# The inverse of the DeltaNet chunk matrices: both heads of a unit in one batch per small-tile step

## The chip, the cores and the metric

The kernel runs on one core of a Trainium2 chip. The core has a matrix engine (TensorE, in profiles PE, with its weight loads as PEld), a vector engine (VectorE, DVE), an activation engine (ScalarE, ACT), a general engine (GpSimd, POOL) and DMA queues, here nearly all issued by SyncE (SP). The engines run their own instruction streams, each in order, and wait for each other through semaphores. Matrix products read SBUF and write PSUM; DVE and ACT bring results from PSUM back to SBUF, which is called an eviction here. The metric is the device time of one execution in microseconds (us).

## What is computed

One decoder layer on 512 tokens of width 2048, in float32. An input projection of the normalised tokens (2048 by 20528) feeds two token mixers, an mLSTM of 8 heads and a gated DeltaNet of 16 heads; an output projection, two sigmoid merge gates, the residual and a final normalisation follow. This is the part of the reference that the change lies in:

```python
    decay_mat = jnp.where(incl, jnp.exp(jnp.where(incl, rel, 0.0)), 0.0)
    kk = jnp.einsum('cbhtd,cbhsd->cbhts', kc, kc)
    a_mat = jnp.where(strict, bc[..., :, None] * kk * decay_mat, 0.0)
    lhs = a_mat + jnp.eye(CHUNK, dtype=a_mat.dtype)
    ...
    sol = lax.linalg.triangular_solve(lhs, rhs, left_side=True, lower=True, unit_diagonal=True)
    w_val, w_k = sol[..., :dv], sol[..., dv:]
    ...
    def step(S, inp):
        wv, wk, qk_c, qd, ke, ge = inp
        u = wv - jnp.einsum('bhtd,bhde->bhte', wk, S)
        o = jnp.einsum('bhtd,bhde->bhte', qd, S) + jnp.einsum('bhts,bhse->bhte', qk_c, u)
        S_new = ge[..., None, None] * S + jnp.einsum('bhsd,bhse->bhde', ke, u)
        return S_new, o
```

For each head and chunk a unit lower triangular matrix has to be inverted (or solved against). The kernel does this with chunks of 128 tokens, so each head has four matrices of 128 by 128.

## The kernel before

**The stream of projections.** The kernel keeps the whole normalised input in SBUF, split in a high and a low part (uh, ul), and streams the weights through in 256 KB pieces. ACT makes the high part of a piece (`wh`, L112), DVE the low part (`wl`, L115), three pieces ahead of use. Each projection product is three TensorE products of 128x512 (L211, L212, L213: high by high, high by low, low by high). TensorE's order is written out by hand: the program issues instructions to it in program order. The other engines are ordered by a scheduler with priorities.

**Ticks.** After each six 128x512 products (or their equal) the projection loop calls `tick()`. All other TensorE work is written as Python generators that are resumed by ticks: a generator does one step's products, requests the evictions and yields the number of ticks after which it wants to go on. So a step's products stand between two projection products, and its eviction has that many ticks before the next step reads it. Every eviction that a later step needs is issued with raised priority (`urgent`).

**Units.** Twelve units follow each other: four mLSTM units ("m") and eight DeltaNet units ("d"), each of two heads, in the order m d d m d d m d d m d d; then come the merge gates and the output projection. A DeltaNet unit projects k, q, v and z for its two heads (64 ticks). `dn_front_k` and `dn_front_q` run beside its own projections: the norms (transposes pkt and pqt), the products k by k and k by q (pk, pqk), and the inverses of the 32x32 diagonal blocks of both heads' eight matrices, solved together on DVE (L530, L532) and brought through DRAM into `tn` (the inverses) and `tt` (their transposes). When the unit's projections are over, `dn_back` starts, beside the projections of the next unit.

**`dn_back` in the kernel before** runs once per head; the second head's generator starts one tick after the first's. It first transposes v (pvt, eviction into `vn`). Then it puts the block inverse together, from 32x32 blocks to 64x64 and then 128x128, in four steps, which use 32x32 and 64x64 tiles of the array:
- p1 (L597): two products a chunk, on two different 32x32 tiles; ACT evicts the negated result into `s1` (L602, one instruction for each of the two partition ranges).
- p2 (L608, L609): three products a chunk, on three different 32x32 tiles; ACT copies two results into `tb` (L613), DVE the third into `ta` (L615).
- p3 (L619): one product a chunk, all on the same 64x64 tile; ACT evicts it into `s3` (L622).
- p4 (L626): one product a chunk, all on the same 64x64 tile; DVE evicts it into `tb` (L628).

Two ticks lie between steps. `tb` then holds the transposed inverse for all four chunks. A float32 product appears as two records in the profile, a transpose as one. There are two sets of `tb` and `ta`, one for each head; POOL puts the diagonal blocks in (L589, L592).

The second half of `dn_back` is the recurrence over the four chunks: pr and the first half of po (state by k and q), the eviction `r` (DVE, L644), pw (L649, reads `tb`), its eviction `w` (ACT, L652), pst and po, the new state (DVE, L660 or L662), two ticks apart each. At the end the result is normalised (squares on ACT, POOL's power `rsd` L676, DVE's multiply `os` L679), transposed seven ticks later (pot, L683) and multiplied by the gate on DVE (`gz`, L686).

PSUM is shared by pools: `psj` (3 tiles) for projections, `psw` (3 tiles, tag "wk") for all the small results, handed out in turn, and `pso` (2 tiles) for po. A small step that gets a "wk" tile waits until the work three tiles back has been evicted.

Of the kernel before, what the change touches and what calls it, by code (L numbers as in the profile page):

```python
# [47 lines left out]
def hybrid_block(  # L48
# [119 lines left out]
    def urgent(level=1):  # L168
        return tc.high_priority(offset=level * PRIO)
# [242 lines left out]
        V.tensor_copy(acol, pc[:, :, 0:8])  # L412
        V.tensor_copy(emcol, pc[:, :, 8:16])

    NYP, NTB = 3, 2
    yps, tbs, tas = [], [], []
    for i in range(NYP):
        t = wk.tile([P, S + 3], F32, tag=f"yp{i}", name=f"yp{i}", bufs=1)
        G.memset(t[:, 0:3], 0.0)
        yps.append(t)  # L420
    for i in range(NTB):
        t = wk.tile([P, NC, P], F32, tag=f"tb{i}", name=f"tb{i}", bufs=1)
        G.memset(t, 0.0)
        tbs.append(t)
        t = wk.tile([64, NC, 64], F32, tag=f"ta{i}", name=f"ta{i}", bufs=1)
        G.memset(t, 0.0)
        tas.append(t)
    cnt = {"yp": 0, "tb": 0}

    def row_bcast(r, name):  # L430
        t = wk.tile([P, NC, P], F32, tag="rb", name=name, bufs=3)
# [134 lines left out]
            u["qt"].append(qt)  # L566
            yield 1

    def dn_back(j, hs, kq, u):
        h = hs[j]  # L570
        aq, qt, ke, ge = u["aq"][j], u["qt"][j], u["ke"][j], u["dm"][j][2]
        nk, qe = u["nk"], u["qe"]

        pv = psw.tile([P, NC, P], F32, tag="wk", name="pvt")
        for c in range(NC):
            T.transpose(pv[:, c, :], u["vt"][j][:, c * P:(c + 1) * P], ident)
        vn = wk.tile([P, NC, P], F32, tag="vn", name="vn", bufs=4)
        with urgent():
            V.tensor_tensor(out=vn, in0=pv, in1=bc(nk[:, j, :], P), op=ALU.mult)
        yield 1  # L580


        tnj, ttj = u["tn"][:, j * NC:(j + 1) * NC, :], u["tt"][:, j * NC:(j + 1) * NC, :]
        tb = tbs[cnt["tb"] % NTB]
        ta = tas[cnt["tb"] % NTB]
        cnt["tb"] += 1
        for b in range(4):
            bs = slice(b * BS, (b + 1) * BS)
            G.tensor_copy(tb[bs, :, bs], ttj[bs])  # L589
        for b in range(2):  # L590
            bs = slice(b * BS, (b + 1) * BS)
            G.tensor_copy(ta[bs, :, bs], tnj[bs])  # L592
        p1 = psw.tile([P, NC, BS], F32, tag="wk", name="p1")
        for q in range(2):
            a0, a1 = slice(64 * q, 64 * q + 32), slice(64 * q + 32, 64 * q + 64)
            for c in range(NC):
                T.matmul(p1[a1, c, :], aq[a0, c, 0, a1], tnj[a0, c, :], start=True, stop=True)  # L597
        s1 = wk.tile([P, NC, BS], F32, tag="s3", name="s1")
        for q in range(2):
            a1 = slice(64 * q + 32, 64 * q + 64)  # L600
            with urgent():
                A.mul(s1[a1], p1[a1], -1.0)  # L602
        yield 2
        p2 = psw.tile([P, 2, NC, BS], F32, tag="wk", name="p2")
        for c in range(NC):
            for q in range(2):
                a0, a1 = slice(64 * q, 64 * q + 32), slice(64 * q + 32, 64 * q + 64)
                T.matmul(p2[a0, 0, c, :], s1[a1, c, :], ttj[a1, c, :], start=True, stop=True)  # L608
            T.matmul(p2[32:64, 1, c, :], ttj[32:64, c, :], s1[32:64, c, :], start=True, stop=True)  # L609
        for q in range(2):  # L610
            a0, a1 = slice(64 * q, 64 * q + 32), slice(64 * q + 32, 64 * q + 64)
            with urgent():
                A.copy(tb[a0, :, a1], p2[a0, 0])  # L613
        with urgent():
            V.tensor_copy(ta[32:64, :, 0:32], p2[32:64, 1])  # L615
        yield 2
        p3 = psw.tile([P, NC, 64], F32, tag="wk", name="p3")
        for c in range(NC):
            T.matmul(p3[64:128, c, :], aq[0:64, c, 0, 64:128], ta[:, c, :], start=True, stop=True)  # L619
        s3 = wk.tile([P, NC, 64], F32, tag="s3", name="s3")  # L620
        with urgent():
            A.mul(s3[64:128], p3[64:128], -1.0)  # L622
        yield 2
        p4 = psw.tile([P, NC, 64], F32, tag="wk", name="p4")
        for c in range(NC):
            T.matmul(p4[0:64, c, :], s3[64:128, c, :], tb[64:128, c, 64:128], start=True, stop=True)  # L626
        with urgent():
            V.tensor_copy(tb[0:64, :, 64:128], p4[0:64])  # L628
        yield 2


        po = pso.tile([P, NC, P], F32, tag="o", name="po")
        ssq = wk.tile([P, NC], F32, tag="ssq", name="ssq")
        st = None
        for c in range(NC):
            tsl = slice(c * P, (c + 1) * P)
            if st is None:
                r = vn[:, c, :]
            else:
                pr = psw.tile([P, P], F32, tag="wk", name="pr")  # L640
                T.matmul(pr, kq[j][:, 0, tsl], st, start=True, stop=True)
                r = wk.tile([P, P], F32, tag="r", name="r")
                with urgent():
                    V.scalar_tensor_tensor(out=r, in0=pr, scalar=negeg[:, c, h:h + 1], in1=vn[:, c, :],  # L644
                                           op0=ALU.mult, op1=ALU.add)
                T.matmul(po[:, c, :], qt[:, c, :], st, start=True, stop=False)
                yield 2
            pw = psw.tile([P, P], F32, tag="wk", name="pw")
            T.matmul(pw, tb[:, c, :], r, start=True, stop=True)  # L649
            w = wk.tile([P, P], F32, tag="w", name="w")  # L650
            with urgent():
                A.copy(w, pw)  # L652
            yield 2
            if c < NC - 1:
                pst = psw.tile([P, P], F32, tag="wk", name="pst")
                T.matmul(pst, ke[:, c, :], w, start=True, stop=True)
                sn = wk.tile([P, P], F32, tag="st", name="st", bufs=4)
                with urgent():
                    if st is None:
                        V.tensor_copy(sn, pst)  # L660
                    else:
                        V.scalar_tensor_tensor(out=sn, in0=st, scalar=ge[:, c:c + 1], in1=pst,  # L662
                                               op0=ALU.mult, op1=ALU.add)
            T.matmul(po[:, c, :], aq[:, c, 1, :], w, start=(st is None), stop=True)
            if c < NC - 1:
                st = sn
                yield 2

        jk = wk.tile([P, P], F32, tag="jk", name="jk", bufs=1)
        for c in range(NC):  # L670
            with urgent():
                A.activation(jk, po[:, c, :], AF.Square, accum_out=ssq[:, c:c + 1])
        with urgent():
            V.scalar_tensor_tensor(out=ssq, in0=ssq, scalar=1.0 / P, in1=qe[:, j, :], op0=ALU.mult, op1=ALU.add)
        rsd = wk.tile([P, NC], F32, tag="rsd", name="rsd")
        G.tensor_tensor(out=rsd, in0=ssq, in1=mhalf, op=ALU.pow)  # L676
        os_ = wk.tile([P, NC, P], F32, tag="os", name="os")
        with urgent():
            V.tensor_tensor(out=os_, in0=po, in1=bc(rsd, P), op=ALU.mult)  # L679
        yield 7  # L680
        pt = psw.tile([P, S], F32, tag="wk", name="pot")
        for c in range(NC):
            T.transpose(pt[:, c * P:(c + 1) * P], os_[:, c, :], ident)  # L683
        ht = u["g"][j]
        with urgent():
            V.scalar_tensor_tensor(out=ht, in0=pt, scalar=normc[:, 32:33], in1=ht, op0=ALU.mult, op1=ALU.mult)  # L686
        nc.sync.dma_start(h_d[KT + h], ht)

    def dn_unit(p):
        hs = (2 * p, 2 * p + 1)  # L690
        dcol = p * NB
        u = {"aq": [], "qt": [], "ke": [], "vt": [], "g": [], "dm": []}
        kq = [wk.tile([P, 2, S], F32, tag="kq", name=f"kq{h}", bufs=4) for h in hs]
        ps = proj_cm(DN_K + dcol)
        for j in range(2):
            conv_silu(ps[j], 16 + hs[j], kq[j][:, 0, :])
        start(dn_front_k(hs, kq, u), KWAIT)
        ps = proj_cm(DN_Q + dcol)
        for j in range(2):
            conv_silu(ps[j], hs[j], kq[j][:, 1, :])  # L700
        start(dn_front_q(hs, kq, u), QWAIT)
        ps = proj_cm(DN_V + dcol)
        for j in range(2):
            vt = wk.tile([P, S], F32, tag="vn", name="vt", bufs=4)
            conv_silu(ps[j], 32 + hs[j], vt)
            u["vt"].append(vt)
        ps = proj_cm(DN_Z + dcol)
        for j in range(2):
            g = wk.tile([P, S], F32, tag="g", name="gz", bufs=4)
            silu2(ps[j], g)  # L710
            u["g"].append(g)
        start(dn_back(0, hs, kq, u), 4)
        start(dn_back(1, hs, kq, u), 5)

    def ml_prep(j, hs, kq, u):
        h = hs[j]
# [280 lines left out]
```

## Time and profile before

| what | value |
|---|---|
| median of 3 runs | 2379.36 us (2378.52 to 2379.41) |
| the profiled execution | 2379.44 us, span 2377.7 us |
| mean granted TensorE clock | 0.998 |
| TensorE (PE) busy | 2344.2 us, 99% of the span |
| DVE, ACT, POOL busy | 1145.5, 826.5, 237.0 us |
| DMA | 265.94 MB, mean 112 GB/s |

The profile is of one execution. The span is from its first to its last instruction; the time of the execution is 1.7 us longer. A group line gives busy time and the mean duration of one instruction; a wait line gives the total, the count and the longest; a timeline line gives the start, the duration, the engine, the line of the kernel, and the idle time before it with what ended it. Products overlap each other, so the pitch of a stream is read from starts, not from durations.

### The profile page before, as it was taken

Reading aid. Unit: us, or ns where it says so; the run is one execution under the profiler, and the core shown is the slowest. Engines: PE = TensorE matmul, PEld = TensorE weight load, DVE = VectorE, ACT = ScalarE, POOL = GpSimd, SP = SyncE. Lnnn points to the kernel's source line nnn. Section 1 sums busy time; section 2 is a strip of 40 time slices with the busy share of each in tenths; the row PEclk is TensorE's granted clock in tenths of the full one; section 3 lists DMA queues with packets and bytes.
Section 4 is the critical chain, followed back from the end, with each engine's and each line's share of the span. In section 5 each row is a group of like instructions: output and inputs, shape, how many; then the busy total and the mean of one; then the engine's idle time right before and its main releaser. Section 6 shows DMA issues by size and latency. Waiting matters only on the chain. (4 is left out here: it accounts for less than half of the span.)

```text
span 2377.7 us, 32465 instructions
## 1 busy us (share of the span) xinstructions
PE 2344.2 (99%) x11999; PEld 1953.4 (82%) x11999; DVE 1145.5 (48%) x2307; ACT 826.5 (35%) x1854; POOL 237.0 (10%) x319
## 2 busy tenths in 40 slices
PE   6999999999999999999999999999999999999998
PEld 5888888888888888888888888888998888888886
DVE  5433767433485833348583324958333222434334
ACT  5323434332343423243343224433333323322222
POOL 0000212100021210011220002112000000010010
PEclk9999999999999999999999999999999999999999
DMA  5433334333333333333342333333375544634333
GB/s 147 114 96 102 94 100 100 94 98 98 98 94 98 107 89 98 97 94 98 96 120 74 107 97 92 96 93 103 91 233 147 159 115 122 207 114 128 121 115 129
DMA packets 232354, 265.94 MB, mean 112 GB/s; under 512 B 46337, under 2 KB 171490, under 8 KB 232194
## 3 DMA queue, kind: packets, MB, share of 16 engines
q1 hardware_dynamic: 232130, 263.79, 39.1%
q8 instruction: 94, 1.54, 0.3%
q14 instruction: 66, 0.54, 0.1%
q10 hardware_dynamic: 64, 0.07, 0.0%
HBM read 239.61 MB, written 24.18 MB: 111 GB/s over the span
## 5 line engine op out<-in xcount | busy, mean ns | idle before, releaser
L115 DVE TENSOR_TENSOR wl<-wr,wh 128x512 fp32r<-128x512 f32 x768 | 550.1, 718 | 875.3 <-ACT wh L112 850.3
L112 ACT CAST wh<-wr 128x512 fp32r<-128x512 f32 x768 | 475.7, 621 | 1148.5 <-PE pj L212 565.4
L211 PE MATMUL pj<-uh,wh 128*128 128x512 f32 x1792 | 736.4, 411 | 2.1 <-ACT yp L442 1.6
L213 PE MATMUL pj<-uh,wl 128*128 128x512 f32 x1792 | 701.4, 391 | 0.0
L212 PE MATMUL pj<-ul,wh 128*128 128x512 f32 x1792 | 699.9, 391 | 0.0
L213 PEld LDWEIGHTS pj<-uh,wl 128*128 128x128 f32 x1792 | 336.5, 188 | 74.5 <-DVE wl L115 0.4
L211 PEld LDWEIGHTS pj<-uh,wh 128*128 128x128 f32 x1792 | 337.4, 188 | 67.1 <-ACT yp L442 2.9
L212 PEld LDWEIGHTS pj<-ul,wh 128*128 128x128 f32 x1792 | 337.9, 189 | 60.5
L935 PE MATMUL py<-wh,hh 128*128 128x512 f32 x512 | 199.2, 389 | 0.0
L936 PE MATMUL py<-wl,hh 128*128 128x512 f32 x512 | 199.2, 389 | 0.0
L937 PE MATMUL py<-wh,hl 128*128 128x512 f32 x512 | 199.2, 389 | 0.0
L241 PE MATMUL pg<-wh,uh 128*128 128x512 f32 x384 | 149.4, 389 | 0.0
L242 PE MATMUL pg<-wl,uh 128*128 128x512 f32 x384 | 149.4, 389 | 0.0
L243 PE MATMUL pg<-wh,ul 128*128 128x512 f32 x384 | 149.4, 389 | 0.0
L936 PEld LDWEIGHTS py<-wl,hh 128*128 128x128 f32 x512 | 96.1, 188 | 20.1
L935 PEld LDWEIGHTS py<-wh,hh 128*128 128x128 f32 x512 | 96.1, 188 | 20.0
L937 PEld LDWEIGHTS py<-wh,hl 128*128 128x128 f32 x512 | 96.1, 188 | 19.8
L241 PE MATMUL pv<-wh,uh 128*128 128x512 f32 x256 | 99.6, 389 | 0.0
L242 PE MATMUL pv<-wl,uh 128*128 128x512 f32 x256 | 99.6, 389 | 0.0
L243 PE MATMUL pv<-wh,ul 128*128 128x512 f32 x256 | 99.6, 389 | 0.0
L530 DVE TENSOR_TENSOR tmp<-ls,xi 32x31 f32<-32x31 f32 (+15 forms) x248 | 91.1, 367 | 5.2 <-DMA ls<-ld 1.7
L532 DVE TENSOR_TENSOR xi<-xi,tmp 32x31 f32<-32x31 f32 (+15 forms) x248 | 87.0, 351 | 4.0
(249 smaller groups left out, 2457.8 us busy)
## 6 DMA issues: line engine op xcount, KB each, us to landing
wr<-in_w_in_dram SPq DMA_DIRECT2D x640, 256.0 KB, 2.8
wr<-in_w_out_dram SPq DMA_DIRECT2D x128, 256.0 KB, 3.1
hr<-h_d SPq DMA_DIRECT2D x32, 256.0 KB, 3.5
tgl<-tg_d SPq DMA_DIRECT2D x32, 256.0 KB, 3.3
tg_d<-tgw SPq DMA_DIRECT2D x24, 256.0 KB, 3.8
xt<-in_x_dram SPq DMA_DIRECT2D x8, 512.0 KB, 9.0
gb<-rows_d SPq DMA_DIRECT2D x16, 256.0 KB, 3.4
h_d<-mg SPq DMA_DIRECT2D x16, 256.0 KB, 3.1
```

The lines of the kernel that those rows point to most:

```text
L112: A.copy(hi, src)
L115: V.tensor_tensor(out=lo, in0=src, in1=hi.bitcast(F32), op=ALU.subtract)
L211: T.matmul(ps[j], hi[:, k, wsl], uh[:, kt, :], start=(kt == 0), stop=False)
L212: T.matmul(ps[j], hi[:, k, wsl], ul[:, kt, :], start=False, stop=False)
L213: T.matmul(ps[j], lo[:, k, wsl], uh[:, kt, :], start=False, stop=(kt == KT - 1))
L241: T.matmul(ps[c], uh[:, kt, tsl], hi[:, 0, :], start=(kt == 0), stop=False)
L242: T.matmul(ps[c], uh[:, kt, tsl], lo[:, 0, :], start=False, stop=False)
L243: T.matmul(ps[c], ul[:, kt, tsl], hi[:, 0, :], start=False, stop=(kt == KT - 1))
L530: V.tensor_tensor(out=tv, in0=ls[:, i, i + 1:BS].unsqueeze(2).to_broadcast([NSYS, n, m]), in1=xi[:, i, 0:m].unsqueeze(1).to_broadcast([NSY ...
L935: T.matmul(ps[c], hh[base][:, kt, tsl], hi[:, 0, :], start=(kt == 0), stop=False)
L936: T.matmul(ps[c], hh[base][:, kt, tsl], lo[:, 0, :], start=False, stop=False)
L937: T.matmul(ps[c], hl[base][:, kt, tsl], hi[:, 0, :], start=False, stop=(kt == KT - 1))
```

## The change

The four steps p1 to p4 are done for both heads of a unit at once. `dn_back` becomes one generator for the unit. It transposes v of head 0 and, a tick later, of head 1; then each of the four steps issues the products of both heads' eight matrices (index `g`) into one PSUM tile and evicts them with the same number of instructions as one head had before, each twice as wide. In p1 the products go to the two array tiles in turn for each matrix, where before all of one tile came first. `tb` and `ta` are single tiles of twice the size, `s1` and `s3` share one buffer. After p4 two generators `dn_chain` are started, one for each head, 2 and 3 ticks later; they hold the recurrence and the rest of the old `dn_back`, unchanged except for the index into `tb`.

```diff
-    NYP, NTB = 3, 2
...
-    for i in range(NTB):
-        t = wk.tile([P, NC, P], F32, tag=f"tb{i}", name=f"tb{i}", bufs=1)
...
+    tb = wk.tile([P, 2 * NC, P], F32, tag="tb", name="tb", bufs=1)
+    G.memset(tb, 0.0)
+    ta = wk.tile([64, 2 * NC, 64], F32, tag="ta", name="ta", bufs=1)
+    G.memset(ta, 0.0)
...
-    def dn_back(j, hs, kq, u):
+    def dn_back(hs, kq, u):
+        u["vs"] = []
+        for j in range(2):
+            pv = psw.tile([P, NC, P], F32, tag="wk", name="pvt")
...
+            u["vs"].append(vn)
+            yield 1
+        tn, tt = u["tn"], u["tt"]
+        G2 = [(j * NC + c, u["aq"][j][:, c, 0, :]) for j in range(2) for c in range(NC)]
...
-        p1 = psw.tile([P, NC, BS], F32, tag="wk", name="p1")
-        for q in range(2):
-            a0, a1 = slice(64 * q, 64 * q + 32), slice(64 * q + 32, 64 * q + 64)
-            for c in range(NC):
-                T.matmul(p1[a1, c, :], aq[a0, c, 0, a1], tnj[a0, c, :], start=True, stop=True)
-        s1 = wk.tile([P, NC, BS], F32, tag="s3", name="s1")
+        p1 = psw.tile([P, 2 * NC, BS], F32, tag="wk", name="p1")
+        for g, a in G2:
+            for q in range(2):
+                a0, a1 = slice(64 * q, 64 * q + 32), slice(64 * q + 32, 64 * q + 64)
+                T.matmul(p1[a1, g, :], a[a0, a1], tn[a0, g, :], start=True, stop=True)
+        s1 = wk.tile([P, 2 * NC, BS], F32, tag="s3", name="s1", bufs=1)
...
+        p2 = psw.tile([P, 2, 2 * NC, BS], F32, tag="wk", name="p2")
+        for g, a in G2:
+            for q in range(2):
+                a0, a1 = slice(64 * q, 64 * q + 32), slice(64 * q + 32, 64 * q + 64)
+                T.matmul(p2[a0, 0, g, :], s1[a1, g, :], tt[a1, g, :], start=True, stop=True)
+            T.matmul(p2[32:64, 1, g, :], tt[32:64, g, :], s1[32:64, g, :], start=True, stop=True)
...
+        p3 = psw.tile([P, 2 * NC, 64], F32, tag="wk", name="p3")
+        for g, a in G2:
+            T.matmul(p3[64:128, g, :], a[0:64, 64:128], ta[:, g, :], start=True, stop=True)
...
+        p4 = psw.tile([P, 2 * NC, 64], F32, tag="wk", name="p4")
+        for g, a in G2:
+            T.matmul(p4[0:64, g, :], s3[64:128, g, :], tb[64:128, g, 64:128], start=True, stop=True)
+        with urgent():
+            V.tensor_copy(tb[0:64, :, 64:128], p4[0:64])
+        start(dn_chain(0, hs, kq, u), 2)
+        start(dn_chain(1, hs, kq, u), 3)
+
+    def dn_chain(j, hs, kq, u):
...
-            T.matmul(pw, tb[:, c, :], r, start=True, stop=True)
+            T.matmul(pw, tb[:, j * NC + c, :], r, start=True, stop=True)
...
-        start(dn_back(0, hs, kq, u), 4)
-        start(dn_back(1, hs, kq, u), 5)
+        start(dn_back(hs, kq, u), 4)
```

More of the change, by code (lines that the diff above doesn't have):

```diff
@@ L413, in gates @@
         V.tensor_copy(emcol, pc[:, :, 8:16])
-    NYP, NTB = 3, 2
-    yps, tbs, tas = [], [], []
+    NYP = 3
+    yps = []
     for i in range(NYP):
@@ L420, in hybrid_block @@
         yps.append(t)
-    for i in range(NTB):
-        t = wk.tile([P, NC, P], F32, tag=f"tb{i}", name=f"tb{i}", bufs=1)
[L423 to L428, printed above, removed]
+    tb = wk.tile([P, 2 * NC, P], F32, tag="tb", name="tb", bufs=1)
+    G.memset(tb, 0.0)
+    ta = wk.tile([64, 2 * NC, 64], F32, tag="ta", name="ta", bufs=1)
+    G.memset(ta, 0.0)
+    cnt = {"yp": 0}
     def row_bcast(r, name):
@@ L567, in dn_front_q @@
             yield 1
-    def dn_back(j, hs, kq, u):
[L570 to L574, printed above, removed]
-        for c in range(NC):
[L576 to L586, printed above, removed]
+    def dn_back(hs, kq, u):
+        u["vs"] = []
+        for j in range(2):
+            pv = psw.tile([P, NC, P], F32, tag="wk", name="pvt")
+            for c in range(NC):
+                T.transpose(pv[:, c, :], u["vt"][j][:, c * P:(c + 1) * P], ident)
+            vn = wk.tile([P, NC, P], F32, tag="vn", name="vn", bufs=4)
+            with urgent():
+                V.tensor_tensor(out=vn, in0=pv, in1=bc(u["nk"][:, j, :], P), op=ALU.mult)
+            u["vs"].append(vn)
+            yield 1
+        tn, tt = u["tn"], u["tt"]
+        G2 = [(j * NC + c, u["aq"][j][:, c, 0, :]) for j in range(2) for c in range(NC)]
@@ L587, in dn_back @@
         for b in range(4):
             bs = slice(b * BS, (b + 1) * BS)
-            G.tensor_copy(tb[bs, :, bs], ttj[bs])
+            G.tensor_copy(tb[bs, :, bs], tt[bs])
         for b in range(2):
             bs = slice(b * BS, (b + 1) * BS)
-            G.tensor_copy(ta[bs, :, bs], tnj[bs])
-        p1 = psw.tile([P, NC, BS], F32, tag="wk", name="p1")
-        for q in range(2):
-            a0, a1 = slice(64 * q, 64 * q + 32), slice(64 * q + 32, 64 * q + 64)
-            for c in range(NC):
-                T.matmul(p1[a1, c, :], aq[a0, c, 0, a1], tnj[a0, c, :], start=True, stop=True)
@@ L598, in dn_back @@
-        s1 = wk.tile([P, NC, BS], F32, tag="s3", name="s1")
+            G.tensor_copy(ta[bs, :, bs], tn[bs])
+        p1 = psw.tile([P, 2 * NC, BS], F32, tag="wk", name="p1")
[4 more added lines that the diff above has]
+        s1 = wk.tile([P, 2 * NC, BS], F32, tag="s3", name="s1", bufs=1)
         for q in range(2):
@@ L603, in dn_back @@
         yield 2
-        p2 = psw.tile([P, 2, NC, BS], F32, tag="wk", name="p2")
-        for c in range(NC):
+        p2 = psw.tile([P, 2, 2 * NC, BS], F32, tag="wk", name="p2")
+        for g, a in G2:
             for q in range(2):
                 a0, a1 = slice(64 * q, 64 * q + 32), slice(64 * q + 32, 64 * q + 64)
-                T.matmul(p2[a0, 0, c, :], s1[a1, c, :], ttj[a1, c, :], start=True, stop=True)
-            T.matmul(p2[32:64, 1, c, :], ttj[32:64, c, :], s1[32:64, c, :], start=True, stop=True)
+                T.matmul(p2[a0, 0, g, :], s1[a1, g, :], tt[a1, g, :], start=True, stop=True)
+            T.matmul(p2[32:64, 1, g, :], tt[32:64, g, :], s1[32:64, g, :], start=True, stop=True)
         for q in range(2):
@@ L616, in dn_back @@
         yield 2
[L617 to L620, printed above, removed]
+        p3 = psw.tile([P, 2 * NC, 64], F32, tag="wk", name="p3")
+        for g, a in G2:
+            T.matmul(p3[64:128, g, :], a[0:64, 64:128], ta[:, g, :], start=True, stop=True)
+        s3 = wk.tile([P, 2 * NC, 64], F32, tag="s3", name="s3", bufs=1)
         with urgent():
@@ L623, in dn_back @@
         yield 2
-        p4 = psw.tile([P, NC, 64], F32, tag="wk", name="p4")
-        for c in range(NC):
-            T.matmul(p4[0:64, c, :], s3[64:128, c, :], tb[64:128, c, 64:128], start=True, stop=True)
+        p4 = psw.tile([P, 2 * NC, 64], F32, tag="wk", name="p4")
+        for g, a in G2:
+            T.matmul(p4[0:64, g, :], s3[64:128, g, :], tb[64:128, g, 64:128], start=True, stop=True)
         with urgent():
             V.tensor_copy(tb[0:64, :, 64:128], p4[0:64])
-        yield 2
+        start(dn_chain(0, hs, kq, u), 2)
+        start(dn_chain(1, hs, kq, u), 3)
+    def dn_chain(j, hs, kq, u):
+        h = hs[j]
+        aq, qt, ke, ge = u["aq"][j], u["qt"][j], u["ke"][j], u["dm"][j][2]
+        qe, vn = u["qe"], u["vs"][j]
         po = pso.tile([P, NC, P], F32, tag="o", name="po")
```

## The prediction

> **What bounds the kernel now.** I read the page first: busy time per engine, and the forty slices.
>
> ```profile
> PE 2344.2 (99%) x11999; PEld 1953.4 (82%) x11999; DVE 1145.5 (48%) x2307; ACT 826.5 (35%) x1854; POOL 237.0 (10%) x319
> PE   6999999999999999999999999999999999999998
> ```
>
> TensorE is busy 99% of the span in every slice but the first and last. "Busy" can hide a wait, so I next asked for everything that TensorE waited for.
>
> ```profile
> PE pprm L102 <- DMA nrow<-in_ml_norm_w_dram: 15.5, 1, 15.5
> PE pqt L551 <- DVE gz L686: 2.1, 4, 0.7
> ...
> PE pj L211 <- ACT yp L442: 1.6, 3, 0.7
> ```
>
> Apart from the first load, the named waits come to a few us in 2378. A change is thus worth what it takes off TensorE's own stream, less any wait that it creates. The third view is the timeline of TensorE around each small-tile step. In steady flow projection products start 0.23 us apart. A small batch stands between two of them; its cost is the start of the second product behind it, less the start of the last one ahead, less two pitches (0.46). Here is the step p3 of one head:
>
> ```profile
> 335.37 0.39 PE L212 MATMUL pj<-ul,wh 128*128 128x512 f32 x1
> 335.60 0.39 PE L213 MATMUL pj<-uh,wl 128*128 128x512 f32 x1
> 335.92 0.67 PE L619 MATMUL p<-ta,aq 64*64 64x64 f32 x8
> 336.53 0.50 PE L211 MATMUL pj<-uh,wh 128*128 128x512 f32 x1
> 336.87 0.39 PE L212 MATMUL pj<-ul,wh 128*128 128x512 f32 x1
> ```
>
> Cost: 336.87 − 335.60 − 0.46 = 0.81 us. The array enters the batch 0.32 after the last product instead of 0.23, and the two pitches behind it are long as well; the records themselves (each float32 product is two) start (0.67 − 0.27)/7 = 0.057 apart. So a batch has a part that is paid once, and a part per record. Step p1 alone, and p2, of which only the start and the resumption are shown:
>
> ```profile
> 329.58 0.40 PE L213 MATMUL pj<-uh,wl 128*128 128x512 f32 x1
> 329.91 0.59 PE L597 MATMUL p<-tn,aq 32*32 32x32 f32 x16
> 330.42 0.50 PE L211 MATMUL pj<-uh,wh 128*128 128x512 f32 x1
> 330.76 0.40 PE L212 MATMUL pj<-ul,wh 128*128 128x512 f32 x1
> ```
>
> ```profile
> 331.68 0.39 PE L213 MATMUL pj<-uh,wl 128*128 128x512 f32 x1
> 332.00 0.22 PE L608 MATMUL p<-tt,s 32*32 32x32 f32 x2
> 332.02 0.21 PE L609 MATMUL p<-s,tt 32*32 32x32 f32 x1
> 332.06 0.20 PE L608 MATMUL p<-tt,s 32*32 32x32 f32 x2
> ...
> 332.38 0.50 PE L211 MATMUL pj<-uh,wh 128*128 128x512 f32 x1
> 332.72 0.40 PE L212 MATMUL pj<-ul,wh 128*128 128x512 f32 x1
> ```
>
> p1: 330.76 − 329.58 − 0.46 = 0.72 for 16 records. p2: 332.72 − 331.68 − 0.46 = 0.58 for 24. The larger batch is the cheaper: p2 deals its products to three tiles of the array in turn, and rounds of three follow every 0.031 us (eight rounds, 0.25), while p1 sends all of one tile first and the other tile's afterwards.
>
> **The change, part by part.** The array work stays: the same products of the same shapes. What changes is how often the stream is broken. Per unit the eight batches (four steps, two heads) become four; in the built order the groups of small products between projection products fall from 384 to 360 (32 batches fewer, but in 8 places p1 shared its gap with pvt, which now stands alone).
>
> *p1.* Before: 0.72 for the head that stands alone; the other shares a gap with pvt, which costs 328.65 − 327.08 − 0.46 = 1.11, less pvt alone (326.15 − 325.25 − 0.46 = 0.44), so 0.67; together 1.39. After: 32 records, dealt to the two tiles in turn, 16 rounds. The nearest row is p2, which has eight such rounds: 0.58 + 8 × 0.031 = 0.83. Saved 0.56. Bounds: if the alternation did nothing, 0.72 + 16 × 0.027 (the mean start pitch of p1 as it is) = 1.15, saved 0.24; 0.56 is also the most. I take 0.56, because p2 shows tiles running side by side.
>
> *p2.* 2 × 0.58 = 1.16 becomes 0.58 + 8 rounds × 0.031 = 0.83. Saved 0.33.
>
> *p3 and p4.* All products of a step use one tile, in series: 2 × 0.81 = 1.62 becomes 0.81 + 8 × 0.057 = 1.27, saved 0.35; p4 (0.80, from 339.99 and 341.25) saves 0.34.
>
> Sum per unit 0.56 + 0.33 + 0.35 + 0.34 = 1.58; eight units, **12.6 us**.
>
> A rule of the Trainium skill speaks against the size of this. "TensorE: Matmul & The Clock Gate", section "Wait — 56ns, not 53.3ns?", says that start to start never drops below about 25 ns however small a product is. By it p2's 24 records would need 0.6 us, where this trace has 0.25; the trace decides. If it held for the longer batches alone, their records would take an estimated 0.8 and 1.2 us, and the saving would be an estimated 4.6 us: rival A, in a sharper form.
>
> *Evictions.* Half as many, twice as wide. ACT's 128-element eviction takes 0.27 and its 256-element one 0.38; DVE's 0.28 and 0.42; for 512 elements the rows of 128x512 copies give 0.62 and 0.69. They lie beside projection products: a step is followed by twelve of them (two ticks) before the next reads its eviction. From p3's end (336.59) that is 0.34 + 10 × 0.23 + 0.32 after 336.53, so 2.9 us. Needed: s1 2 × 0.38 = 0.8; the longest, p2: 0.06 + two ACT copies 0.76 + 0.03 + DVE 0.42 = 1.3; s3 0.7; the last DVE copy 0.75. Cover 1.6 us or more, so I cost them at nothing; were the cover gone, each us would be paid 32 times. The two heads no longer fill each other's ticks, so the interval is shorter than before (2.9 instead of 3.7, from 336.59 to p4's start at 340.31), but long enough. ACT's split of the next weights (0.62) becomes due at the same tick, ahead of the batch, and is over when the batch ends.
>
> *Buffers.* One tb, ta and s1/s3 instead of two. POOL's twelve diagonal copies (0.29 each) become six wider ones, and the first product that reads them is p3, four ticks behind p1. A unit's tb is written again 64 ticks later, after its last reader (the recurrences end some 31 ticks on). Nothing.
>
> *The chain one tick later.* Both heads' recurrences start one tick later, 14 and 15 ticks after the unit's last projection instead of 13 and 14, keeping their offset. From 14 on, ticks that held one head's work hold the other's, so the waits of pr, pw and pst keep their budgets of two ticks. One place changes: in the four units followed by another DeltaNet unit, pot falls onto the next unit's pqt. There TensorE already waits today:
>
> ```profile
> 394.57 0.60 PE L683 MATMUL pot<-ident,os 128*128 128x128 f32 x4
> 395.65 0.66 PE L551 MATMUL pqt<-ident,kq 128*128 128x128 f32 x4 [0.48 <-DVE gz L686]
> ```
>
> pqt starts 1.08 after pot instead of 0.44: 0.64 lost, because its PSUM tile is freed by DVE's multiply gz (394.87, 0.73 long). In the changed order pot of head 0 meets the second pqt, and it is pqk that waits for gz. With the first pot at 392.30 as zero, pqk is due at 1.83 + 2.27 + 0.44 = 4.5 (pqt had been due at 2.7). gz now ends at 3.3; in the new order of DVE it has five solve steps (L530, L532; 0.36 apart) more and one L445 (0.66) less ahead of it since os, so +1.2, and os comes 0.5 to 1.6 later (its own DVE backlog, or a full tick): gz ends at 5.0 to 6.1. Lost 0.5 to 1.6 where 0.64 is lost now; times four, +0.6 gained to 3.8 us lost. I take no change, near the end where os is set by DVE's backlog, as now.
>
> *Sum.* The profiled execution took 2379.44 us (span 2377.7), the median of the runs 2379.36; 2379.4 − 12.6 = **2366.8 us**, 0.53% less. A measurement of this kernel can tell about 0.2%, 4.8 us.
>
> **The rivals.** *A. Long batches run short of instructions or of issue.* TensorE's queue is seen working ahead (it passes the p4 wait at 337.12 for a product at 340.31), 17 records in between (nine projection products and eight of p3). If records beyond that came at one per 0.032, the p1 batch would take 0.25 more and p2 0.66 more: 0.9 per unit, 7.3 in all: 2374.1. Against: p2's 24 records already exceed 17 and keep their pace to the end; for: no batch of 48 is in the trace.
>
> *B. The tail of the solve.* gz stands behind still more work than counted, by one tick: 2.3 lost in place of 0.64, four times: 2366.8 + 6.6 = 2373.4. For: DVE runs without a gap from os to gz there. Against: the order is fixed and its list counted.
>
> *C. The eviction takes the place of the gap: slower.* One step of both heads ends in one eviction that all next products need; if it takes longer than 2.9 us, TensorE stands. The gain is lost at a wait of 12.6/32 = 0.39 per step, and slower by 0.2% begins at (12.6 + 4.8)/32 = 0.54. Were the two splits (0.62 on ACT, 0.69 on DVE) and two 128x512 activations (0.7) queued ahead of p2's eviction at every step, it would take 1.3 + 2.7 = 4.0, a wait of 1.1, 32 times 35 us: 2402. Against: evictions start 0.04 to 0.4 after their products today, and the heavy work for DVE and ACT (convolution, squares) begins at tick 16, behind p4. The Trainium skill has this rule, "TensorEngine Tiling (Array Packing)", section "PSUM Bottleneck": tiling speeds up TensorE, not the evacuation of PSUM, which may become the bottleneck. No row here shows it doing so.
>
> *D. The change does nothing.* The order shows the 32 batches gone, so only an unpaid fixed part could make it so; the fixed part (0.58 − 0.25 = 0.33 in p2) is in every batch above. Taken as excluded but for the unforeseen.
>
> **How the numbers follow.** Forecast with its bounds (2363 to 2371: the 0.64 waits may also vanish, 2.6 us; a small batch may be off by 0.03, 1 us): 0.77. A 0.08, B 0.06, C 0.05, the unforeseen 0.04, half of it slower. The range must reach past B and A, so 2363 to 2374.5. Faster by over 0.2% (below 2374.6): the forecast, B and most of A, 0.86. Within 0.2%: some of A and of the unforeseen, 0.07; slower: C and the rest, 0.07.
>
> **What would show it.** Right: the timeline has p1, p2, p3, p4 of 32, 48, 16, 16 records at costs of about 0.83, 0.83, 1.27, 1.26; no wait of these lines on s, ta or tb in TensorE's list; a pqk wait on gz of some 0.3 to 1.6, four times. Wrong: a batch whose records slow down behind the 17th (A), a wait of pqk over 2 us (B), or waits of the small products on ACT and DVE evictions (C).

## The result and the profile after

| | before | after |
|---|---|---|
| median | 2379.39 us (2378.52 to 2379.90, 6 runs) | 2363.56 us (2363.21 to 2363.77, 6 runs) |
| span of the profiled execution | 2377.7 | 2361.9 |

The ratio is 0.9934, interval [0.9924, 0.9945]: 15.8 us less, in the runs and in the profiled spans alike. The forecast was 2366.8, 12.6 less. The page's line of busy times, and then all that TensorE waited for (us in total, times, longest):

```profile
PE 2330.6 (99%) x11999; PEld 1950.0 (83%) x11999; DVE 1134.5 (48%) x2291; ACT 819.3 (35%) x1814; POOL 230.2 (10%) x269
```

```profile
PE pprm L102 <- DMA nrow<-in_ml_norm_w_dram: 16.3, 1, 16.3
...
PE pqk L557 <- DVE gz L686: 0.7, 4, 0.2
PE pj L211 <- ACT wh L112: 0.4, 1, 0.4
...
```

As many matmul records as before (11999), 13.6 us less of busy time. The wait on gz has moved from pqt to pqk and is a third as long, 0.7 for 2.1; the waits of L211 on yp (1.6 before) are gone from the list; no small-tile step waits for s, ta or tb. The weight load of L211 waits for yp as well, and there less than half of the wait is left, before and after:

```profile
PEld pj L211 <- ACT yp L442: 2.9, 3, 1.1
```

```profile
PEld pj L211 <- ACT yp L439: 1.3, 3, 0.5
```

Now the batches in TensorE's timeline: p1 with its 32 records, p3 with 16, and p2, of which only the ends are shown.

```profile
328.98 0.40 PE L213 MATMUL pj<-uh,wl 128*128 128x512 f32 x1
329.31 0.69 PE L592 MATMUL p<-tn,aq 32*32 32x32 f32 x32
...
330.26 0.40 PE L212 MATMUL pj<-ul,wh 128*128 128x512 f32 x1
...
336.12 0.39 PE L213 MATMUL pj<-uh,wl 128*128 128x512 f32 x1
336.44 1.14 PE L614 MATMUL p<-ta,aq 64*64 64x64 f32 x16
...
337.85 0.39 PE L212 MATMUL pj<-ul,wh 128*128 128x512 f32 x1
```

```profile
332.55 0.39 PE L213 MATMUL pj<-uh,wl 128*128 128x512 f32 x1
332.87 0.22 PE L603 MATMUL p<-tt,s 32*32 32x32 f32 x2
...
333.38 0.19 PE L604 MATMUL p<-s,tt 32*32 32x32 f32 x1
...
333.84 0.40 PE L212 MATMUL pj<-ul,wh 128*128 128x512 f32 x1
```

By the prediction's rule for the cost of a batch p1 costs 0.82, p2 0.83, p3 1.27; p4 the same 1.27. The 48 records of p2 start within 333.38 − 332.87 = 0.51 us. Each batch is entered 0.32 to 0.33 after the last product and left with two long pitches, as it was before at half the length: that part is now paid once per step and not twice.

Where the 15.8 us lie, from the start times of the same projection product in both traces, summed over stretches:

| stretch | saved, us |
|---|---|
| small-tile steps of eight units (1.63 each in the first unit of a pair, 1.66 to 1.71 in the second) | 13.2 |
| around pqt and pqk, four times | 1.25 |
| from there to past the start of a second unit's v projection, four times | 1.63 |
| all the rest | −0.3 |

The second row is the wait on gz. The third lies in three of the four places (0.75, 0.58, 0.30 and nothing). The prediction had not named it: there L211 waited for ACT's copy yp.

### The profile page after: what moved, and what is told of

It is laid out like the page before. It is cut to its first block, busy times and chain, and to the rows that moved or that the text cites. A ratio compares the mean times of both kernels' runs of the same rounds, so it can differ in the third digit from the quotient of the medians.

```text
span 2361.9 us, 32309 instructions
## 1 busy us (share of the span) xinstructions
PE 2330.6 (99%) x11999; PEld 1950.0 (83%) x11999; DVE 1134.5 (48%) x2291; ACT 819.3 (35%) x1814; POOL 230.2 (10%) x269
## 4 chain that ended last, share of the span: by engine, by line
PE 96%; DVE 2%; POOL 1%; issue 0%; DMA 0%; ACT 0%; SPq 0%; POOLq 0%; DVEq 0%
PE pj L211 17%; PE pj L213 17%; PE pj L212 17%; PE py L934 5%; PE py L936 5%; PE py L935 5%; PE pg L242 4%; PE pg L243 4%; PE pg L241 4%; PE pv L241 2%; PE pv L243 2%; PE pv L242 2%; PE pjt L226 1%; PE pjt L229 1%; PE pjt L228 1%; PE pqk L557 1%
## 5 line engine op out<-in xcount | busy, mean ns | idle before, releaser
L115 DVE TENSOR_TENSOR wl<-wr,wh 128x512 fp32r<-128x512 f32 x768 | 544.5, 710 | 899.6 <-ACT wh L112 871.4
L211 PE MATMUL pj<-uh,wh 128*128 128x512 f32 x1792 | 733.6, 409 | 0.5 <-ACT wh L112 0.4
L211 PEld LDWEIGHTS pj<-uh,wh 128*128 128x128 f32 x1792 | 337.2, 188 | 65.1 <-ACT yp L439 1.3
```

What stands on the lines that cost most here:

```text
L115: V.tensor_tensor(out=lo, in0=src, in1=hi.bitcast(F32), op=ALU.subtract)
L211: T.matmul(ps[j], hi[:, k, wsl], uh[:, kt, :], start=(kt == 0), stop=False)
```

## The experiments

The table gives medians; "saved" is against the kernel before in the same comparison. Ratios stand with their intervals in the text. The kernel before had medians from 2379.0 to 2380.1 in these comparisons, so medians of different comparisons that are less than 1 us apart do not tell two kernels apart; the start times in the traces resolve more.

| kernel | us | before, us | saved |
|---|---|---|---|
| before + p1 in turn | 2377.22 | 2380.07 | 2.9 |
| after, p1 tile by tile | 2367.02 | 2379.33 | 12.3 |
| after + 24 extra breaks | 2373.45 | 2379.33 | 5.9 |
| after, a tile and evictions per head | 2363.54 | 2380.07 | 16.5 |
| after, one tick between steps | 2364.04 | 2379.33 | 15.3 |
| before, a tick later | 2377.35 | 2380.07 | 2.7 |
| after, a tick earlier | 2365.61 | 2380.07 | 14.5 |
| after, pot later | 2362.98 | 2379.33 | 16.4 |
| after, em in its own tiles | 2364.35 | 2379.02 | 14.7 |
| the same, pot later | 2372.11 | 2379.02 | 6.9 |
| before, em in its own tiles | 2380.04 | 2379.02 | −1.0 |
| after, pot later, em behind q | 2360.91 | 2379.53 | 18.6 |

### What a batch costs

**The kernel before, p1's products dealt to the tiles in turn.**

```diff
-        for q in range(2):
-            a0, a1 = slice(64 * q, 64 * q + 32), slice(64 * q + 32, 64 * q + 64)
-            for c in range(NC):
+        for c in range(NC):
+            for q in range(2):
+                a0, a1 = slice(64 * q, 64 * q + 32), slice(64 * q + 32, 64 * q + 64)
                 T.matmul(p1[a1, c, :], aq[a0, c, 0, a1], tnj[a0, c, :], start=True, stop=True)
```

> The kernel before, with only the order of p1's products changed: chunk by chunk to the two array tiles in turn. Theory (two tiles of the array work side by side, a round each 0.031 us): a p1 batch of 16 records costs 0.58 instead of 0.72, 16 batches, 2.2 us less: 2377.2. Rival (p1 is bound by its records, whichever tile they go to): 2379.4.

Ratio 0.9988 [0.9980, 0.9997]. In its timeline the batch that stood at 0.72 costs 329.79 − 328.75 − 0.46 = 0.58, as p2 with its 24 records did:

```profile
328.75 0.40 PE L213 MATMUL pj<-uh,wl 128*128 128x512 f32 x1
329.08 0.44 PE L597 MATMUL p<-tn,aq 32*32 32x32 f32 x16
...
329.79 0.40 PE L212 MATMUL pj<-ul,wh 128*128 128x512 f32 x1
```

0.147 per batch, sixteen batches, 2.4 us: the order alone, with as many batches as before.

**The changed kernel, p1 one tile after the other.**

```diff
-        for g, a in G2:
-            for q in range(2):
+        for q in range(2):
+            for g, a in G2:
```

> The changed kernel with p1's 32 records sent to one array tile first and then to the other. Theory (tiles side by side): the batch costs 1.15 instead of 0.83, if the mean pitch of 0.027 of the p1 of before holds, eight times: 2.6 us more, 2366.2. The first tile's 16 records may also all have to pass before the second tile's overlap: up to 0.83 + 0.5, 4 us more. Rival (bound by records): no change, 2363.6.

Ratio 0.9946 [0.9934, 0.9959]; 3.5 us above the change. The batch has the same 32 records as in the change and takes 1.09 for 0.69:

```profile
329.36 0.40 PE L213 MATMUL pj<-uh,wl 128*128 128x512 f32 x1
329.69 1.09 PE L592 MATMUL p<-tn,aq 32*32 32x32 f32 x32
...
331.04 0.40 PE L212 MATMUL pj<-ul,wh 128*128 128x512 f32 x1
```

Its cost, 331.04 − 329.36 − 0.46 = 1.22, is even above the 1.15 that the prediction set for "alternation did nothing". So of p1's 0.56 a unit, 0.40 hangs on the order of its products: 3.2 to 3.5 of the change's 15.8 us come from the new order in p1, which the change brings along with the joining.

**The changed kernel with 24 lone products.** In each of the three waits between the steps one 32x32 product into a PSUM tile of its own; its output is not used.

```diff
-        yield 2
+        yield 1
+        pd = pso.tile([P, BS], F32, tag="o", name="pd")
+        T.matmul(pd[32:64, :], tn[0:32, 0, :], tn[0:32, 0, :], start=True, stop=True)
+        yield 1
```

> The changed kernel with one extra 32x32 product (two records, its result is not used) put alone between the steps, one tick behind p1, p2 and p3: 24 extra breaks of the stream. Theory (a break of the projection stream by a small-tile batch costs a fixed 0.33 us, plus 0.03 a record round): 0.33 + 0.06 each, 24 times, 9.4 us more: 2373.0. Rival (the gain was records or evictions, a break itself is cheap): 24 times 0.06, 1.4 us more, 2365.0.

Ratio 0.9974 [0.9964, 0.9984]. The profile puts 1.21 us on each unit, 0.405 per break; 24 × 0.405 = 9.7 of the 9.9 us between the two medians. The two records of one product cost 331.34 − 330.51 − 0.46 = 0.37 here:

```profile
330.51 0.39 PE L213 MATMUL pj<-uh,wl 128*128 128x512 f32 x1
330.83 0.24 PE L600 MATMUL pd<-tn 32*32 32x32 f32 x2
...
331.34 0.40 PE L212 MATMUL pj<-ul,wh 128*128 128x512 f32 x1
```

**The changed kernel with a PSUM tile and evictions per head** (both heads still in one batch a step):

```diff
-        p3 = psw.tile([P, 2 * NC, 64], F32, tag="wk", name="p3")
-        for g, a in G2:
-            T.matmul(p3[64:128, g, :], a[0:64, 64:128], ta[:, g, :], start=True, stop=True)
...
+        for j in range(2):
+            p3 = psw.tile([P, NC, 64], F32, tag="wk", name="p3")
+            for g, c, a in GS[j]:
+                T.matmul(p3[64:128, c, :], a[0:64, 64:128], ta[:, g, :], start=True, stop=True)
```

> The changed kernel, but each head keeps its own PSUM tile and its own evictions in each step; the products of both heads still follow each other without a projection product in between. Theory (only the number of gaps in TensorE's stream counts; evictions are covered): as the change, 2363.6, within 1 us. Rival (one PSUM tile and one eviction for both heads are part of the gain): 2 us or more above it.

Ratio 0.9931 [0.9918, 0.9945], as the change. The shared PSUM tile and the single eviction are worth nothing that can be measured; the shared break remains, and the order in p1, which this kernel has too.

**The changed kernel with one tick between the steps**, begun later so that the end stays where it was:

```diff
-        yield 2
+        yield 1
...
-        start(dn_back(hs, kq, u), 4)
+        start(dn_back(hs, kq, u), 7)
```

> The changed kernel with one tick instead of two between p1, p2, p3 and p4, and dn_back started three ticks later, so that the recurrences stand as in the change. The next step then follows some 1.5 us behind the end of the one whose eviction it reads; needed by the prediction: 0.8, 1.3 and 0.7 us. Theory: no wait in most units, 2363.6, at most 0.3 us at p3, 2.4 more, where a weight split stands ahead of the eviction. Rival C of the prediction (the evictions are near to binding): 0.5 us or more at each of 24 steps, 12 us more, 2376.

Ratio 0.9934 [0.9920, 0.9947], as the change, and no step waits. The tightest place, in DVE's timeline and then in TensorE's: ta is evicted until 337.27 + 0.42 = 337.69, and p3 starts on time at 337.95.

```profile
337.27 0.42 DVE L610 COPY ta<-p 32x256 f32<-32x256 f32 x1 [0.30 <-ACT tb L608]
```

```profile
337.64 0.39 PE L213 MATMUL pj<-uh,wl 128*128 128x512 f32 x1
337.95 1.14 PE L614 MATMUL p<-ta,aq 64*64 64x64 f32 x16
```

With half the cover 0.26 us are left, in this unit and in the others. Rival C needed a wait of 0.39 a step, with twice this cover, to use up the gain.

### What the tick is worth

**The kernel before, its steps and recurrences a tick later; the change, a tick earlier.**

```diff
-        start(dn_back(0, hs, kq, u), 4)
-        start(dn_back(1, hs, kq, u), 5)
+        start(dn_back(0, hs, kq, u), 5)
+        start(dn_back(1, hs, kq, u), 6)
```

> The kernel before, with both heads' dn_back started one tick later (5 and 6 instead of 4 and 5): no batch is merged, only the recurrences stand where the change puts them. Theory (the 3 us beyond the predicted 12.6 come from the tick): the pqt wait of 0.7 becomes a pqk wait of 0.45, and the wait for yp where the second unit's v projection starts (1.0, 0.9, 0.6 us) falls to 0.3; together 2.9 us less, 2376.5 us. Rival (the extra comes from the fewer evictions, which free ACT and DVE): no change, 2379.4.

```diff
-        start(dn_back(hs, kq, u), 4)
+        start(dn_back(hs, kq, u), 3)
```

> The changed kernel with dn_back started at tick 3 instead of 4, so that the recurrences stand where they stood before. Theory: the merged batches alone, 13.2 us less than before, with the old pqt waits of 0.7 and the old yp waits of 0.6 to 1.0: 2366.2 us. Rival (fewer evictions free ACT and DVE): as the change, 2363.5.

Ratios 0.9990 [0.9981, 0.9999] and 0.9940 [0.9928, 0.9953]. The tick by itself saves 2.7 us (1.6 in the profiled execution, where one row came late at the v projection). Without it the change loses 1.3 us, when each of the two is set against the kernel before of its own comparison (15.8 and 14.5 saved), and 1.3 in the profiled spans. The list of the second kernel has both waits back:

```profile
PE pqt L548 <- DVE gz L686: 1.9, 4, 0.5
PE pj L211 <- ACT yp L439: 0.9, 3, 0.3
```

So the later tick, a side effect of taking the heads together, is worth 1.3 to 2.7 us of the 15.8, and the batches about 13.

### What is late next, and a faster version

**The changed kernel, pot two ticks later.**

```diff
-        yield 7
+        yield 9
         pt = psw.tile([P, S], F32, tag="wk", name="pot")
```

> The changed kernel with nine ticks instead of seven between the last eviction of the recurrence and pot, so that pot comes behind pqt and pqk instead of among them. Theory (pqk waits because its PSUM tile is held by pot until gz has read it): the four waits of 0.44 go, 1.8 us less, 2361.8, if the order on DVE leaves the yp wait at 0.3. Rival (the wait is DVE's backlog and moves to the next user): 2363.6.

Ratio 0.9929 [0.9917, 0.9942]: 0.6 us below the change, between the two expectations and too little for these medians to show. The traces are clearer: the wait on gz is gone, worth 2.05 more around pqt and pqk, but the v stretch gives 1.8 back. ACT's timeline ahead of the copy yp in one of the pairs, and the product of TensorE that waits for it:

```profile
807.60 1.28 ACT L723 ACTIVATE em<-em,acol 128x128 f32<-128x128 f32 x4 [3.83 <-POOL em L720]
808.78 0.60 ACT L112 CAST wh<-wr 128x512 fp32r<-128x512 f32 x1
809.29 0.57 ACT L439 COPY yp<-pj 128x512 f32<-128x512 f32 x1
```

```profile
809.92 0.50 PE L211 MATMUL pj<-uh,wh 128*128 128x512 f32 x1 [1.20 <-ACT yp L439]
```

ACT stands still for 3.8 us in front of exponentials of em, the mask of the mLSTM unit to come, which the built order has put ahead of yp. They wait for POOL's select, POOL waits for a row (nrb), and the row is asked for late. POOL's and then SP's timeline of the same stretch:

```profile
801.18 0.76 POOL L720 TENSOR_SCALAR_AFFINE_SELECT em<-nrb 128x512 f32<-128x512 f32 x1 [2.42 <-DVE aq L560]
...
806.91 0.65 POOL L720 TENSOR_SCALAR_AFFINE_SELECT em<-nrb 128x512 f32<-128x512 f32 x1 [3.09 <-DMA nrb<-rows_d]
```

```profile
801.96 0.34 SPq L429 DMA_DIRECT2D nrb<-rows_d  x1
```

The first em takes over the tile dm that aq (L560) gives up; its select frees the row's tile, and only then SP asks for the second row, at 801.96; it is there at 806.9. So aq, which pqk feeds, sets through four hands when TensorE may begin the v projection.

**em and nrb in a tag of their own,** in the change, in the change with pot later, and in the kernel before (in the second, pot is two ticks later as above: the 9 of its expectation is the argument of the yield).

```diff
-        rb = row_bcast(h, "nrb")
+        rb = row_bcast(h, "nrb", wp, "tg")
...
-        em = wk.tile([P, NC, P], F32, tag="dm", name="em")
+        em = wp.tile([P, NC, P], F32, tag="tg", name="em", bufs=3)
```

> The changed kernel with the mLSTM mask tiles em and nrb taken from the SBUF tag tg, which is free in this phase, and no longer from dm and rb; nothing of the DeltaNet steps differs. Theory (at the start of a second d unit's v projection TensorE waits for the copy yp because ScalarE's exponentials of em stand ahead of it, and these wait for a row that is fetched only once the DeltaNet eviction aq has released dm): with tiles of its own em is done long before, and the wait of L211 on yp, 0.9 us in the three pairs of the changed kernel's profile (0.3, 0.3, 0.3, none), goes: 2362.7 us, and no wait of pj on yp above 0.1 us. Rival (the wait is that of the PSUM buffer itself, whatever stands ahead on ScalarE): 2363.6 us, the waits stay at 0.3.

> As the kernel with em's own tiles, and with pot's products handed out 9 ticks later, so that the eviction gz is done before TensorE reaches pqk. Theory (the two waits are separate, and the later pot gained little alone because it delayed aq and with it em): the waits on gz, 0.44 us four times, and those on yp, 0.9 us in all, both go: 2363.56 - 0.9 - 1.8 = 2360.9 us. Rival (what pot later gains is given back at the v projection by another wait): 2362.5 to 2363.0 us.

> The kernel before, with em and nrb taken from the tag tg. Theory: the waits of the v projection on yp in the profile before, 1.0, 0.9, 0.6 and 0 = 2.5 us, go, and nothing else: 2379.4 - 2.5 = 2376.9 us; 1.6 of the change's 15.8 us were then a part of this wait and not of the small-tile steps. Rival (the wait is that of the PSUM buffer): 2379.4 us.

The theory missed all three: ratios 0.9938 [0.9925, 0.9950], 0.9970 [0.9959, 0.9981] and 1.0004 [0.9995, 1.0013], that is the change's time or a little more, 8.5 us more than the change, and the time of before. The first two expectations also start from a wait of the matmul that the change's list does not have; what it has is the wait of the weight load, 1.3 in all. The third time is the one that its rival gave, but not by the rival's cause: there too the exponential of gb stands ahead of yp, and the matmul's waits on yp grow from 1.6 to 2.4. em's exponentials are indeed gone from there. ACT's timeline of the first shows what came in their place, and the waits of TensorE in the second what it came to:

```profile
807.71 0.63 ACT L470 ACTIVATE gb<-gb 128x512 f32<-128x512 f32 x1 [4.55 <-POOL dm L468]
...
808.76 0.98 ACT L474 ACTIVATE dm<-dm,ngam 128x128 f32<-128x128 f32 x3
809.65 0.56 ACT L439 COPY yp<-pj 128x512 f32<-128x512 f32 x1
```

```profile
PE pj L211 <- ACT yp L439: 6.3, 3, 2.3
```

The tiles rb and dm that em left free were taken by the masks of the next DeltaNet unit (gb, dm), whose exponential needs a row just as fresh. With pot later this row is asked for only behind gz's store, in SP's order of the second kernel:

```profile
806.43 0.34 SPq L687 DMA_DIRECT2D h_d<-gz  x1
806.83 0.77 SPq L429 DMA_DIRECT2D gb<-rows_d  x1
```

The exponential starts at 811.6 there, and TensorE waits 2.3 us. These waits are little more than half of what this kernel loses. By the start times it loses 3.8, 4.1 and 3.7 us in three v stretches, 11.7 in all (and gains 2.0 at gz), with waits of 2.0, 2.3 and 2.0. Behind each of the three the granted clock (PEclk, as a share of full speed) falls to a half for 3.4 us, and products start 0.43 apart where 0.23 is usual. The view of stretches gives from and to, the length, each engine's busy time and then PEclk; here one of the three, and the stretch behind it:

```profile
core 0: us, PE busy (x) PEld busy (x) DVE busy (x) ACT busy (x) POOL busy (x), PEclk, DMA share, GB/s
815.40:818.80 3.40, 3.40 (x9) 2.63 (x9) 3.40 (x7) 0.83 (x2) 0.00 (x0) 0.50 0.31 94
818.80:822.00 3.20, 3.20 (x15) 2.63 (x15) 3.20 (x9) 1.04 (x2) 0.00 (x0) 1.00 0.31 89
```

Half the speed for 3 × 3.4 us is worth 5.1 us, which with the 6.3 of the waits makes 11.4 of the 11.7. The wait of 1.7 us in the kernel before with the later tick was not followed by such a stretch. A buffer given to one tile thus moved the hoisting on to the next; what the three misses share is that something that waits for a row stands ahead of yp.

**em behind its own unit's q.** A true dependency keeps the exponentials from being handed out early, and the tiles stay taken:

```diff
         em = wk.tile([P, NC, P], F32, tag="dm", name="em")
+        G.tensor_copy(em[:, 0, 0:1], qT[:, 0:1])
```

> The changed kernel with pot's products two ticks later (yield 9 for 7, as in the experiment on pot alone), and with the first column of em written by GpSimd from the mLSTM unit's own qT before the mask is made: em then can't be made, and its exponentials can't be handed to ScalarE, before that unit's q projection is done, so that nothing that waits for a row stands ahead of the copy yp at the start of a second d unit's v projection. Theory (whatever waits for a row ahead of yp on ScalarE is what TensorE pays there; in the kernels with em's own tiles the exponential of gb had only taken em's place): both waits go, on gz and on yp, 1.8 us for the first as with pot later alone and 1.3 us for its waits on yp, and the longest wait of pj on yp is under 0.2 us: 2362.98 - 1.3 = 2361.7 us. Rival (yp is late by its own PSUM buffer or the copies wh, not by what waits for rows): 2363.0 us, with waits on yp as with pot later alone, 0.1, 1.2, 0 and 0.1.

Ratio 0.9921 [0.9908, 0.9935]: 2360.91 us (2360.39 to 2361.33), 2.1 below pot later alone and 2.65 below the change. ACT's timeline at the same place holds nothing but weights and yp, which now waits for its own product (and not TensorE for it):

```profile
804.21 0.62 ACT L112 CAST wh<-wr 128x512 fp32r<-128x512 f32 x1 [2.56 <-PE pj L212]
805.79 0.59 ACT L439 COPY yp<-pj 128x512 f32<-128x512 f32 x1 [0.96 <-PE pj L213]
```

Of TensorE's waits all that is left in the list is:

```profile
PE pprm L102 <- DMA nrow<-in_ml_norm_w_dram: 15.8, 1, 15.8
PE put L290 <- DVE xt L283: 2.0, 1, 2.0
PE pj L211 <- ACT wh L112: 0.4, 1, 0.4
PE pgt L333 <- ACT gr L317: 0.3, 1, 0.3
```

The v stretch gained 2.27 over pot later alone, more than the 1.2 of its matmul's wait: the weight loads of L211, which wait for yp as well, had stood 2.6 us in three pairs there and do not wait for it here. The rival is out: the copies wh still stand ahead of yp, and its PSUM buffers are the same.

## Why the prediction was right, and where it was off

*The batches.* Right, term by term. Predicted 0.83, 0.83, 1.27, 1.26; in the seven places where each stands alone they cost 0.82, 0.83, 1.27, 1.27. The sum 1.58 a unit became 1.63 to 1.71, 13.2 for 12.6 in all; what makes up the 0.05 to 0.13 beyond the batches was not followed. p1's size was the boldest step, since it took its pace from another step (p2) and not from p1 as it was; the two experiments on its order bear it out from both sides. That the fixed part is paid per break, however little stands in it, is shown by the lone products: 0.37 to 0.38 each, of which the prediction's 0.33 is the fixed part.

*Rival A.* Out. The batches of 32 and 48 records cost what the prediction's pace of 0.031 a round gives, to 0.01 us; none slows down behind the 17th. The trace also disagrees with the page of the Trainium skill that stood beside it ("TensorE: Matmul & The Clock Gate", section "Wait — 56ns, not 53.3ns?", 25 ns from start to start at the least): 48 records, dealt to three tiles, start in 0.51 us, 0.011 apart. On any one of the tiles they are 0.031 apart; that a floor of this size holds for one tile is not contradicted here.

*Evictions and rival C.* Costed at nothing, rightly. The longest need was put at 1.3; in the change p2's evictions end 334.82 − 333.57 = 1.25 after its last record, 1.6 ahead of p3. With one tick in place of two they still do not bind. What "TensorEngine Tiling (Array Packing)", section "PSUM Bottleneck", of the Trainium skill warns of did not come about here, at half the cover either.

*gz: the term that was mis-sized.* The mechanism was right: the wait passed to pqk, four times. Taken as unchanged 0.64, with 0.5 to 1.6 as bounds, it measures 395.62 − 394.83 − 0.44 = 0.35, below the lower bound:

```profile
394.83 0.60 PE L683 MATMUL pot<-ident,os 128*128 128x128 f32 x4
395.62 1.16 PE L557 MATMUL pqk<-kq 128*128 128x128 f32 x8 [0.19 <-DVE gz L686]
```

DVE's timeline has the second head's os, and gz, in the kernel after, and then os in the kernel before (gz at 394.87 there):

```profile
388.22 0.69 DVE L679 TENSOR_TENSOR os<-po,rsd 128x512 f32<-128x512 f32 x1 [0.30 <-POOL rsd L676]
...
394.83 0.73 DVE L686 SCALAR_TENSOR_TENSOR gz<-pot,normc,gz 128x512 f32<-128x512 f32 x1
```

```profile
389.51 0.69 DVE L679 TENSOR_TENSOR os<-po,rsd 128x512 f32<-128x512 f32 x1 [0.30 <-POOL rsd L676]
```

The count of DVE's work between os and gz held: gz starts 6.61 after os (394.83 − 388.22), 5.36 before, 1.25 more for the 1.2 counted. What failed is "os comes 0.5 to 1.6 later": from the stream's zero (392.30 before, 390.75 after) os stands at −2.79 before and −2.53 after, only 0.26 later. The prediction took os to be set by DVE's backlog; in both rows DVE stands idle for 0.30 in front of it and waits for POOL's rsd. Rival B (2.3) was far off.

*What was not in the sum.* The 1.6 us at the v projection. The prediction showed the waits on yp in its second view, did not ask what decides them, and wrote "One place changes", which was the place at pqt. In the trace before, as in the change, it is em's row: relative to the start of the stretch aq stands 0.7 earlier in the change, the second nrb is asked for 0.7 earlier, and yp comes so early that the matmul of L211 no longer waits and its weight load waits less. The kernel before with the tick alone showed the same in two of its pairs (0.78 and 0.33 saved) and the opposite in a third (1.14 lost, the row landing late): this part rests on a DMA and varies.

*Rival D.* Out: the breaks taken away were paid, and lone breaks put back were paid again.

Forecast and result differ by 3.2 us. In the profile the gz term makes 1.25 of it, the yp waits 1.6, the batches 0.6, the rest −0.3. The three parts all point the same way, so none hid another; the result stands 0.6 us above the lower end of the range (2363), which the prediction had drawn for the gz waits and not for yp.

## What to carry to other kernels

Where a full array runs without gaps, price small-tile products by break and not by product: count how often the stream leaves its shape, take the break's price from the trace (here 0.33 to 0.4 us), join independent small work in one break, and deal its products to the tiles in turn. A merge also moves everything behind it in time, so ask of each named wait next to it what sets it, through every buffer and queue. Giving a tile a buffer of its own changes what the scheduler may hoist; where something that waits for a DMA must not stand ahead of an eviction, here a true dependency held it back and a spare buffer did not. And price a long wait of TensorE at more than its length: here each of three waits of about 2 us was followed by 3.4 us at half the granted clock.

## What the runs showed of the hardware that was not expected

- The order of small products matters beside their number: 32 records on two 32x32 tiles cost 0.82 us in turn and 1.22 tile by tile; 16 cost 0.58 and 0.72.
- A single 32x32 product (two records) between full-array products costs 0.37 to 0.38 us, about as much as 1.6 projection products of 0.23.
- A row of 256 KB had a median of 3.8 us from issue to landing (nrb, with pot later), but where it mattered 4.95 passed until POOL could start on it (801.96 to 806.91). ACT, which stood in front of em's exponentials, passed that on to TensorE as a wait of 1.2 us.
- Waits of TensorE of 2.0, 2.3 and 2.0 us were each followed by 3.4 us at a granted clock of 0.50; a wait of 1.7 us was not.
